# First-layer shift columns on TensorE, fewer GpSimd splits, and four memory units at each change of stage

## The chip, the cores and the metric

One core of one Trainium2 chip runs the whole program as one launch. The metric is the device time in microseconds of that core. Engines go by their names: TensorE (PE, with its weight loads as PEld), VectorE (DVE), ScalarE (ACT), GpSimd (POOL) and SyncE (SP).

## What is computed

Two chained blocks over x of 256 tokens by 1024 channels. The first block has two layers (retention with a PEER feed-forward, then a spatial gating unit with another); each norm is modulated by columns that come from the vector c. The second block adds a hybrid of attention and convolution, cross-attention to a memory, and an MLP. What the change touches is this part (cut):

```python
def rmsnorm(x, gain):
    x32 = x.astype(jnp.float32)
    y = x32 * lax.rsqrt(jnp.mean(x32 * x32, axis=-1, keepdims=True) + EPS)
    return (y * gain.astype(jnp.float32)).astype(x.dtype)

def modulate(h, shift, scale):
    return h * (1 + scale[:, None, :]) + shift[:, None, :]
```

The columns `shift` and `scale` (and four others for each layer) are silu(c) times a 1024 x 6144 matrix `ada_w` plus a bias. The memory's keys and values are projections of the normed memory (256 x 1024), needed only in the second block.

## The kernel before

All activations are held with channels on partitions, as 8 tiles of 128x256. Every weight matrix comes as units of 512 KB (128x1024 f32). `plan` (L204 on) lays them down as one list, in the order in which they are used. `pump` walks the list: it issues loads on SyncE's queue into four `raw` buffers (and eight `early` buffers for the first modulation units), then turns each unit into two halves: ScalarE copies it to the high half (L285), and VectorE, or GpSimd where the plan's `on_pool` marks the unit, subtracts to give the low half (L287). `get` hands a split unit to TensorE; `f1` and `f2` run three fp32r matmuls for each product (L320 to L322, L353 to L355). Up to three split units are held.

An "ada" unit of the list gives one modulation column of 128 channels: VectorE multiplies the 128x1024 unit by `cact`, which is silu(c) in every partition, and sums along the row (L292). After eight of them a bias is added (L296). So eight units make the shift and eight the scale of a norm.

`run` (L536 on) starts the program: it loads `vecs`, `mem`, `craw` (c in every partition) and `x`; ScalarE and VectorE split the memory into `mh` (tiles `h`); `mem_values` runs the eight units `mem_v` into four accumulators `pmv`, with sixteen modulation units of the first layer placed between them in the list. The steps handed to `pipe` run behind each unit: the squares of x and of the memory (`ms_add`, whose sums GpSimd adds at L407), the rotary tables, the root of x. Sums over channels are matmuls with `ones` into `st`.

`retention` begins with `mod_gain` and `apply`: for each of eight tiles VectorE makes `t` (L464), ScalarE the high half of `h` (L465), VectorE the low half (L467). Then come the units `ret_qk` into `pqk`. The memory's root is finished inside retention (`mem_stats`).

The same norm stands at each later change of stage: at `peer(0)`, `sgu` and `peer(1)`. While VectorE and ScalarE work on it, TensorE runs units of `mem_k` (`mem_keys`, into `pmk`): three, three and two. `ms_finish` takes the sum, root and reciprocal behind the first of them. The query units `pq` follow through `f1_pair`.

The order on each engine is the order in which this code issues instructions; nothing is sorted later. DMA issues stand in the queue of the engine that issues them.

Of the kernel before, what the change touches and what calls it, by code (L numbers as in the profile page):

```python
# [10 lines left out]
F32 = mybir.dt.float32  # L11
# [5 lines left out]
AF = mybir.ActivationFunctionType  # L17
# [5 lines left out]
P = 128  # L23
T = 256
D = 1024
# [67 lines left out]
def _layout(x):  # L93
# [10 lines left out]
                                   "g_mlp_2", "g_final_2", "conv_w_2")]  # L104
    o["vecs"] = np.concatenate(vecs, axis=1)
    o["ada"] = x["ada_w"].transpose(0, 2, 1).reshape(2, 48, P, D)
# [39 lines left out]
for _n, _w in (("norm_mix", 16), ("norm_ffn", 16), ("norm_final", 8), ("ada_b", 96), ("sgu_b", 24),  # L146
               ("ln_g", 24), ("ln_b", 24),
               ("g_mix", 8), ("g_attn", 4), ("g_conv", 4), ("g_xattn", 8), ("g_mem", 8), ("g_mlp", 8),
               ("g_final", 8), ("conv_w", 12)):
    VEC[_n] = (_off, _w)  # L150
    _off += _w


class Net:
# [41 lines left out]
    def plan(self):  # L196
# [29 lines left out]
        mk = ws(a["mem_k"], "mem_k")  # L226
# [31 lines left out]
    def pump(self, ahead, spare=None):  # L258
        nc = self.nc
        while self.w_split < self.w_done + ahead and self.n_split < len(self.units):  # L260
            i = self.n_split
            while self.n_load < len(self.units):
# [3 lines left out]
                early = ada and j < 24  # L266
# [12 lines left out]
            self.flying[unit[0] == "ada" and i < 24] -= 1  # L279
# [63 lines left out]
    def f2(self, pss, hs, tag, after=None):  # L343
        mm = self.nc.tensor.matmul
        for q in range(4):
# [49 lines left out]
    def ms_add(self, src):  # L395
# [131 lines left out]
    def run(self):  # L527
# [25 lines left out]
        mem = ps.tile([P, KC, T], F32, name="mem")  # L553
        nc.scalar.dma_start(self.vecs, a["vecs"])
# [8 lines left out]
        iota = ps.tile([P, P], F32, name="iota_all")  # L563
        self.const(iota, "iota")
        self.cs = pf.tile([P, 2, T], F32, name="cs")
        rope = self.rope(ps, self.cs)
# [7 lines left out]
        self.cact = self.p_n.tile([P, D], F32, tag="cact", name="cact")  # L574
        nc.scalar.activation(self.cact, cr, AF.Silu)
        nc.gpsimd.dma_start(self.d_c, self.cact[0:1, :])
        self.ms_begin(KC)
        nc.vector.tensor_copy(self.iota, iota[:, :TOPK])
        nc.vector.tensor_copy(self.iota_rep, iota[:, :, None].to_broadcast([P, P, 2]))
        def squares(src, n):  # L580
            return lambda: [self.ms_add(src[:, n + k]) for k in range(4)]
        st = {}

        def total():
            st[0] = self.ms_root(self.ms_sum(), KC)
            self.ms_begin(KC)

        def rstd():
# [7 lines left out]
        self.fill_pool, self.fill_h = cm_f, mh  # L596
# [14 lines left out]
    def mem_values(self, mh):  # L611
        nc = self.nc
        pss = [self.acc_tile("pmv") for _ in range(4)]
        for g in range(2):
            self.f2(pss[2 * g:2 * g + 2], mh, "mem_v", self.tick)
        self.drain()

        def store(g):
            for tb in range(2):
                o = self.p_n.tile([P, 512], F32, tag="mo", name="mo", bufs=2)  # L620
                nc.scalar.activation(o, pss[2 * g + tb], AF.Copy)
                nc.gpsimd.dma_start(self.d_mv[:, tb, g * 512:g * 512 + 512], o)
        return store

    def mem_keys(self, mh, count, mid=None):
        nc = self.nc
        for k in range(count):
            h = len(self.mem_pend) % 2
            if h == 0:
                self.mem_ps = self.acc_tile("pmk")  # L630
            pt = self.mem_ps[:, h * T:h * T + T]
            self.f1(pt, self.get("mem_k"), mh, mid=mid if k == 0 else None)
            self.mem_pend.append((pt, self.mem_n))
            self.mem_n += 1

    def mem_stores(self):
        nc = self.nc
        while self.mem_pend:
            pt, n = self.mem_pend.popleft()
            o = self.p_n.tile([P, T], F32, tag="mk", name="mk", bufs=3)  # L640
            nc.scalar.activation(o, pt, AF.Copy)
            nc.gpsimd.dma_start(self.d_mk[:, n], o)
# [60 lines left out]
    def retention(self, rstd):  # L703
        nc = self.nc
        gain = self.mod_gain(0, "norm_mix", 8)
        hs = self.apply(rstd, gain, self.mod[0][:, 0:8], {4: lambda: self.mem_store_v(0)})
        self.later.append(lambda: self.mem_store_v(1))
# [119 lines left out]
    def peer(self, l):  # L827
        nc, a = self.nc, self.a
        gain = self.mod_gain(l, "norm_ffn", 32)
        def more():  # L830
            self.mem_keys(self.fill_h, 1)
        self.mem_keys(self.fill_h, 1, self.ms_finish)
        more()
        hs = self.apply(self.rstd, gain, self.mod[l][:, 24:32], {1: more, 6: lambda: self.pump(SPLIT_BUFS)} if l == 0 else {6: lambda: self.pump(SPLIT_BUFS)})
# [87 lines left out]
        def reopen(cm_g):  # L922
# [13 lines left out]
            if l == 0:  # L936
                self.fill_h = self.mem_reload(pf, nc.sync)
# [285 lines left out]
    def sgu(self):  # L1223
        nc, a = self.nc, self.a
        gain = self.mod_gain(1, "norm_mix", 8)
        def more():
            self.mem_keys(self.fill_h, 1)
        self.mem_keys(self.fill_h, 1, self.ms_finish)
        more()
        hs = self.apply(self.rstd, gain, self.mod[1][:, 0:8], {1: more, 6: lambda: self.pump(SPLIT_BUFS)})  # L1230
# [113 lines left out]
        def swap():  # L1344
# [3 lines left out]
            self.fill_h = self.mem_reload(pf, nc.gpsimd)  # L1348
# [446 lines left out]
```

## Time and profile before

| | us |
|---|---|
| median of 3 runs | 2589.46 |
| lowest, highest | 2589.04, 2594.5 |
| profiled execution | 2594.92 |
| its span, first to last instruction | 2593.1 |
| TensorE busy | 2505.1 (97%) |
| VectorE busy | 1905.0 (73%) |
| ScalarE busy | 1258.9 (49%) |
| GpSimd busy | 303.2 (12%) |

The profile is of one execution; its steps are read as durations and starts within the span. A record of a matmul begins before the one ahead of it has ended, so the cost of one in a row is the distance of the starts, not its own length. An fp32 matmul leaves two records. The granted clock of TensorE is given as a share of full speed.

### The profile page before, as it was taken

The page shows a single profiled execution, that of the slowest core. Times are in us where ns is not written, and L with a number is a line of the kernel's source. Part 1 is how long each engine was busy: PE and PEld are TensorE (multiplying, and loading weights), DVE is VectorE, ACT ScalarE, POOL GpSimd, SP SyncE. Part 2 cuts the span into 40 slices and gives each one's busy share as a digit, 9 for nine tenths or more (in the row PEclk, how much of TensorE's full clock was granted, in tenths as well). Part 3 has the DMA queues.
Part 4 walks back from the last instruction along what each step waited for, and adds up shares of the span by engine and source line. Part 5 has one row for each costly group of instructions (what it writes and reads, how often), then busy time and mean ns, then how long its engine had stood idle before and what let it go on. Part 6 is the DMA issues. An engine that isn't in the chain of part 4 may idle for free.

```text
span 2593.1 us, 49906 instructions
## 1 busy us (share of the span) xinstructions
PE 2505.1 (97%) x20358; PEld 2441.9 (94%) x20358; DVE 1905.0 (73%) x3190; ACT 1258.9 (49%) x1790; POOL 303.2 (12%) x210
## 2 busy tenths in 40 slices
PE   5999999999999999999999999999999999989998
PEld 3989999999999999988999999999999999889998
DVE  8777688888868667775776888888675555785754
ACT  4435444444444444455545444444444444665543
POOL 5000312200001000020133222000100000111001
PEclk8999999999999999999999999999999999999999
DMA  7685555555569788867565555555775655444553
GB/s 290 217 300 166 196 174 184 181 182 189 193 219 308 252 301 274 272 224 247 168 203 174 176 183 184 181 190 195 255 249 181 217 187 181 148 134 158 169 193 115
DMA packets 146407, 532.34 MB, mean 205 GB/s; under 512 B 16081, under 2 KB 18257, under 8 KB 145281
## 3 DMA queue, kind: packets, MB, share of 16 engines
q1 hardware_dynamic: 133104, 481.36, 55.9%
q0 software_dynamic: 11584, 45.56, 4.8%
q8 instruction: 160, 2.62, 0.4%
q10 hardware_dynamic: 1488, 2.23, 0.2%
q14 instruction: 71, 0.57, 0.1%
HBM read 506.93 MB, written 22.16 MB: 204 GB/s over the span
## 4 chain that ended last, share of the span: by engine, by line
PE 81%; DVE 9%; DMA 4%; ACT 4%; issue 2%; POOL 1%; DVEq 0%; ACTq 0%; SPq 0%; POOLq 0%
PE pu L320 11%; PE pu L321 11%; PE pu L322 11%; PE V L321 9%; PE V L322 9%; PE V L320 9%; PE po L321 3%; PE po L322 3%; PE po L320 3%; DVE split L287 3%; PE g L1161 2%; ACT split L285 2%; PE pq L321 1%; PE pq L322 1%; PE pq L320 1%
## 5 line engine op out<-in xcount | busy, mean ns | idle before, releaser
L287 DVE TENSOR_TENSOR split<-raw,split 128x1024 fp32r<-128x1024 f32 x740 | 907.9, 1230 | 558.8 <-ACT split L285 558.1
L285 ACT ACTIVATE split<-raw 128x1024 fp32r<-128x1024 f32 x808 | 850.8, 1057 | 711.1 <-PE V L322 334.8
L320 PE MATMUL pu<-h,split 128*128 128x256 f32 x2496 | 718.4, 288 | 0.1
L321 PE MATMUL pu<-h,split 128*128 128x256 f32 x2496 | 706.5, 283 | 0.5 <-DVE h L380 0.5
L322 PE MATMUL pu<-h,split 128*128 128x256 f32 x2496 | 705.9, 283 | 1.1 <-POOL split L287 0.9
L322 PE MATMUL V<-a_sp,split 128*128 128x256 f32 x2048 | 579.9, 283 | 3.6 <-DVE split L287 3.6
L320 PE MATMUL V<-a_sp,split 128*128 128x256 f32 x2048 | 579.9, 283 | 1.2 <-ACT split L285 1.2
L321 PE MATMUL V<-a_sp,split 128*128 128x256 f32 x2048 | 580.1, 283 | 0.1
L321 PEld LDWEIGHTS pu<-h,split 128*128 128x128 f32 x2496 | 478.5, 192 | 1.3 <-DVE h L380 0.7
L322 PEld LDWEIGHTS pu<-h,split 128*128 128x128 f32 x2496 | 478.0, 192 | 1.7 <-POOL split L287 1.3
L320 PEld LDWEIGHTS pu<-h,split 128*128 128x128 f32 x2496 | 478.1, 192 | 0.6 <-ACT u L1328 0.3
L322 PEld LDWEIGHTS V<-a_sp,split 128*128 128x128 f32 x2048 | 393.0, 192 | 4.2 <-DVE split L287 4.2
L320 PEld LDWEIGHTS V<-a_sp,split 128*128 128x128 f32 x2048 | 393.0, 192 | 1.6 <-ACT split L285 1.6
L321 PEld LDWEIGHTS V<-a_sp,split 128*128 128x128 f32 x2048 | 392.9, 192 | 0.5 <-DVE a_sp L374 0.5
L287 POOL TENSOR_TENSOR split<-raw,split 128x1024 fp32r<-128x1024 f32 x68 | 175.3, 2579 | 553.7 <-ACT split L285 551.5
L878 ACT ACTIVATE S<-pu 128x512 f32<-128x512 f32 x128 | 76.5, 597 | 234.8 <-PE pu L322 234.8
L292 DVE SCALAR_TENSOR_TENSOR raw<-raw,cact 128x1024 f32<-128x1024 f32 x96 | 126.8, 1327 | 3.2 <-DMA raw<-in_ada 1.6
L407 POOL TENSOR_TENSOR ms_acc<-ms_acc,sq 128x256 f32<-128x256 f32 x45 | 51.1, 1135 | 571.5 <-ACT sq L405 568.7
L1153 DVE TENSOR_TENSOR og<-og,g 128x512 f16<-128x512 f16 x256 | 108.8, 425 | 8.8
L1171 ACT ACTIVATE stage<-g 128x256 f32<-128x256 f32 x128 | 48.8, 382 | 109.6 <-DVE S L1167 109.6
L320 PE MATMUL pq<-h,split 128*128 128x256 f32 x320 | 95.9, 300 | 3.5 <-ACT h L465 1.9
L321 PE MATMUL pq<-h,split 128*128 128x256 f32 x320 | 93.6, 292 | 4.7 <-DVE h L467 3.2
(370 smaller groups left out, 4018.2 us busy)
## 6 DMA issues: line engine op xcount, KB each, us to landing
raw<-in_pu SPq DMA_DIRECT2D x256, 512.0 KB, 3.3
raw<-in_pv SPq DMA_DIRECT2D x256, 512.0 KB, 4.2
raw<-in_ada SPq DMA_DIRECT2D x96, 512.0 KB, 4.7
raw<-in_pq SPq DMA_DIRECT2D x32, 512.0 KB, 3.3
d_g<-stage POOLq DMA_DIRECT2D x32, 512.0 KB, 3.8
g<-d_g POOLq DMA_DIRECT2D x16, 1024.0 KB, 9.5
raw<-in_mlp_u SPq DMA_DIRECT2D x32, 512.0 KB, 3.4
raw<-in_mlp_d SPq DMA_DIRECT2D x32, 512.0 KB, 4.0
```

The source lines that it names most:

```text
L285: nc.scalar.activation(s[:, 0], r, AF.Copy)
L287: eng.tensor_sub(s[:, 1], r, s[:, 0].bitcast(F32))
L292: nc.vector.scalar_tensor_tensor(r, r, 1.0, self.cact, op0=ALU.mult, op1=ALU.mult, accum_out=self.mod[l][:, o:o + 1])
L320: mm(ps, w_hi, x_hi, start=start, stop=False, **kw)
L321: mm(ps, w_hi, x_lo, start=False, stop=False, **kw)
L322: mm(ps, w_lo, x_hi, start=False, stop=stop, **kw)
L407: nc.gpsimd.tensor_add(self.ms_parts[0], self.ms_parts[0], sq)
L878: nc.scalar.activation(S[:, i - 1:i + 1], pt, AF.Gelu_apprx_tanh)
L1153: nc.vector.tensor_tensor(og[:, k], og[:, 1], pairs(g3[:, k, tt]), op=ALU.mult)
L1161: nc.tensor.matmul(g[:, t], o1[:, t // 2, :, t % 2], og[:, k, t // 2, :, t % 2], start=k == 0, stop=k == 1)
L1171: nc.scalar.activation(stage[0][:, :, k * GT:k * GT + GT], g[:, 64:], AF.Copy)
```

## The change

The first eight units of `ada` are laid out as blocks of matmul weights. They go through ScalarE's DMA queue into a tile `wc` and are multiplied with silu(c) held as a column (`c_col`) by 64 fp32 matmuls with one moving column, into `pmod`; VectorE adds the bias. The scale's eight units stay as they were. At the start only four of the eight `mem_v` units run; the other four run at `peer(0)`, four `mem_k` at `sgu`, and four at `peer(1)`. A new function `bridge` places them. `on_pool` is dropped for the units beside these norms and for `mem_v` and `ret_qk`, and `ms_add` adds on VectorE. At the start the squares come four times as 128x512 into `sq_all`, each root is eight matmuls, and the memory's root is taken there, so that `mem_stats` keeps a reciprocal. The rotary steps `turns` and `reduce` come first.

```diff
-        mix(on_pool(ws(a["mem_v"], "mem_v"), 2, 4, 6), cols(0, 0, 16), 2)
-        mix(on_pool(ws(a["ret_qk"], "ret_qk"), 0, 1, 3))
+        mix(mv[:4], cols(0, 8, 16), 2)
+        mix(ws(a["ret_qk"], "ret_qk"))
...
-        mix(mk[:3])
+        mix(mv[4:])
         for l in range(2):
             pq = ws(a["pq"][16 * l:16 * l + 16], "pq")
-            mix(on_pool(pq, 0, 1, 2, 4, 7, 10, 13))
+            mix(on_pool(pq, 4, 7, 10, 13))
...
-                mix(on_pool(mk[3:6], 2))
-                mix(on_pool(ws(a["sgu_v"], "sgu_v"), 0, 1, 2) + on_pool(ws(a["sgu_u"], "sgu_u"), *range(0, 24, 4)), cols(1, 37, 48), 1, 6)
+                mix(mk[:4])
+                mix(ws(a["sgu_v"], "sgu_v") + on_pool(ws(a["sgu_u"], "sgu_u"), *range(0, 24, 4)), cols(1, 37, 48), 1, 6)
                 mix(ws(a["sgu_o"], "sgu_o", 4))
-                mix(mk[6:8])
+                mix(mk[4:])
...
-            nc.gpsimd.tensor_add(self.ms_parts[0], self.ms_parts[0], sq)
+            nc.vector.tensor_add(self.ms_parts[0], self.ms_parts[0], sq)
...
         nc.scalar.dma_start(self.vecs, a["vecs"])
+        nc.scalar.dma_start(cr, a["c"].to_broadcast([P, D]))
+        rope = self.rope(ps, self.cs)
         for k in range(2):
             nc.sync.dma_start(mem[:, 4 * k:4 * k + 4], a["memT"][:, 4 * k:4 * k + 4])
-        cr = ps.tile([P, D], F32, name="craw")
-        nc.scalar.dma_start(cr, a["c"].to_broadcast([P, D]))
+        nc.scalar.dma_start(wc[:, 0], a["ada"][0])
         nc.scalar.dma_start(self.x, a["xT"])
+        for k in range(1, KC):
+            nc.scalar.dma_start(wc[:, k], a["ada"][k])
...
+        def columns(*ks):
+            for k in ks:
+                w = wc[:, k].rearrange("p (c m) -> p c m", m=P)
+                for c in range(KC):
+                    nc.tensor.matmul(pmod[:, k:k + 1], w[:, c], c_col[:, c:c + 1], start=c == 0, stop=c == KC - 1,
+                                     skip_group_check=True)
...
+        def root():
+            ps = self.st_tile("st")[:, :T]
+            for n in range(KC):
+                nc.tensor.matmul(ps, self.ones, sq[:, n], start=n == 0, stop=n == KC - 1)
+            st[0] = self.ms_root(ps, KC)
...
+        def first():
+            nc.vector.tensor_copy(self.iota, iota[:, :TOPK])
+            nc.vector.tensor_copy(self.iota_rep, iota[:, :, None].to_broadcast([P, P, 2]))
+            columns(1, 2)
+            squares(self.x)
+            rope[2]()
+
+        def second():
+            root()
             self.rstd = self.ms_recip(st[0], "rstd")
-        self.pipe([squares(self.x, 0), lambda: (rope[0](), squares(self.x, 4)()), rope[1],
-                   lambda: (rope[2](), total(), squares(mem, 0)()), rstd, squares(mem, 4)])
-        self.mem_store_v = self.mem_values(mh)
+            columns(3, 4)
+            squares(mem)
+
+        def third():
+            columns(5, 6)
+            root()
+
+        columns(0)
+        self.pipe([first, second, third, lambda: (columns(7), shift())])
+        self.mem_values(mh, 0, self.tick)
...
     def mem_stats(self):
-        r = self.rsqrt(self.ms_sum(), KC, "mrstd")
+        r = self.ms_recip(self.mem_root, "mrstd")
...
+    def bridge(self, gain, shift):
+
+        fill = self.fill
+        fill.popleft()()
+        self.ms_finish()
+        fill.popleft()()
+        hs = self.apply(self.rstd, gain, shift, {1: fill.popleft(), 3: fill.pop(), 6: lambda: self.pump(SPLIT_BUFS)})
+        fill.clear()
+        return hs
```

ScalarE's queue at the start of the program, with the semaphores each instruction waits for. A name such as `DMAHW1` is one of the eight semaphores that all loads of the SyncE and ScalarE queues use in turn. Before:

```order
L554 DMA vecs<-in_vecs 128x268
L558 DMA craw<-in_c 128x1024
L559 DMA x<-in_xT 128x2048
L378 ACT_TABLE_LOAD [waits DMAHW1_49]
L378 ACTIVATE h<-mem,vecs 128x256 [waits DMAHW0_49]
L378 ACTIVATE h<-mem,vecs 128x256 x3
L378 ACTIVATE h<-mem,vecs 128x256 [waits DMAHW3_49]
```

After:

```order
L560 DMA craw<-in_c 128x1024
L564 DMA wc<-in_ada 128x1024
L565 DMA x<-in_xT 128x2048
L567 DMA wc<-in_ada 128x1024 [waits DMAHW1_49]
L567 DMA wc<-in_ada 128x1024 [waits DMAHW3_49]
L567 DMA wc<-in_ada 128x1024 [waits DMAHW5_49]
L567 DMA wc<-in_ada 128x1024 [waits DMAHW7_49]
...
L575 ACT_TABLE_LOAD
L575 ACTIVATE c_col<-vecs 128x8 [waits DMAHW0_49]
L577 ACTIVATE cact<-craw 128x1024 [waits DMAHW2_49]
L379 ACTIVATE h<-mem,vecs 128x256 x8
L286 ACTIVATE split_194<-raw_170 128x1024
```

Seven loads of `wc` (three of them where the dots stand), each with a wait, now stand ahead of the first activation; `c_col` and `cact` moved ahead of the memory's `h`.

VectorE at the first change of stage, from retention to PEER (`x` is the residual, `split` a low half, `rstd` the reciprocal of the root). Before:

```order
L476 SCALAR_TENSOR_TENSOR gain<-mod_80,vecs 128x8
L287 TENSOR_TENSOR split_2538<-raw_2425,split_2538 128x1024
L441 RECIPROCAL rstd<-rs 128x256
L464 SCALAR_TENSOR_TENSOR t<-x,gain,rstd 128x256 x2
L467 SCALAR_TENSOR_TENSOR h<-t,mod_80,h 128x256
L464 SCALAR_TENSOR_TENSOR t<-x,gain,rstd 128x256
```

After:

```order
L477 SCALAR_TENSOR_TENSOR gain<-mod_80,vecs 128x8
L288 TENSOR_TENSOR split_2492<-raw_2378,split_2492 128x1024
L442 RECIPROCAL rstd<-rs 128x256
L288 TENSOR_TENSOR split_2518<-raw_2411,split_2518 128x1024
L465 SCALAR_TENSOR_TENSOR t<-x,gain,rstd 128x256 x2
L468 SCALAR_TENSOR_TENSOR h<-t,mod_80,h 128x256
L288 TENSOR_TENSOR split_2546<-raw_2444,split_2546 128x1024
L465 SCALAR_TENSOR_TENSOR t<-x,gain,rstd 128x256
L468 SCALAR_TENSOR_TENSOR h<-t,mod_80,h 128x256
L465 SCALAR_TENSOR_TENSOR t<-x,gain,rstd 128x256
L468 SCALAR_TENSOR_TENSOR h<-t,mod_80,h 128x256
L288 TENSOR_TENSOR split_2571<-raw_2490,split_2571 128x1024
```

Between the reciprocal and the last `h` stood no split on this engine; now four stand there (three of them shown).

## Rows read from the trace of the kernel before

**Rows 1.** The page's busy shares and its chain that ended last.
```profile
PE 2505.1 (97%) x20358; PEld 2441.9 (94%) x20358; DVE 1905.0 (73%) x3190; ACT 1258.9 (49%) x1790; POOL 303.2 (12%) x210
...
PE 81%; DVE 9%; DMA 4%; ACT 4%; issue 2%; POOL 1%; DVEq 0%; ACTq 0%; SPq 0%; POOLq 0%
```
**Rows 2.** Waits of TensorE, 0 to 130 us: total, times, longest.
```profile
PE pqk L320 <- ACT h L465: 5.6, 1, 5.6
...
PE pqk L322 <- POOL split L287: 1.3, 1, 1.3
```
**Rows 3.** Chain that ended last, 0 to 80 us: start, length, what.
```profile
10.18 10.89 DMA raw<-in_mem_v
...
59.22 2.19 DVE mod L296
61.44 0.18 DVE gain L476
...
62.16 0.52 ACT h L465
```
**Rows 4.** ScalarE's timeline at the start: start, length, operation.
```profile
5.49 1.28 ACT L378 ACT_TABLE_LOAD   x1 [5.49 <-DMA mem<-in_memT]
6.78 1.70 ACT L378 ACTIVATE h<-mem,vecs 128x256 fp32r<-128x256 f32 x4
...
15.62 1.06 ACT L575 ACTIVATE cact<-craw 128x1024 f32<-128x1024 f32 x1
```
**Rows 5.** Waits of SyncE's queue, 0 to 40 us.
```profile
SPq L273 <- DMA craw<-in_c: 3.4, 1, 3.4
```
**Rows 6.** Windows of the start: length, each engine, PEclk, DMA share, GB/s.
```profile
16.00:24.00 8.00, 7.55 (x24) 5.59 (x23) 7.29 (x10) 3.72 (x6) 2.27 (x2) 1.00 1.03 420
...
40.00:48.00 8.00, 5.21 (x14) 3.35 (x12) 8.00 (x11) 6.68 (x13) 4.26 (x4) 0.75 0.47 171
```
**Rows 7.** VectorE's timeline in the start: two modulation units.
```profile
40.88 1.22 DVE L292 SCALAR_TENSOR_TENSOR raw<-raw,cact 128x1024 f32<-128x1024 f32 x1
...
55.79 3.39 DVE L292 SCALAR_TENSOR_TENSOR raw<-raw,cact 128x1024 f32<-128x1024 f32 x1
```
**Rows 8.** TensorE's timeline: memory units at the start, fp16 matmuls in layer 0.
```profile
22.68 0.40 PE L354 MATMUL pmv<-split,h 128*128 128x512 f32 x1
22.91 0.40 PE L355 MATMUL pmv<-split,h 128*128 128x512 f32 x1
...
532.80 0.51 PE L1161 MATMUL g<-og,o 128*128 128x128 f16 x6
533.11 0.36 PE L320 MATMUL pu<-h,split 128*128 128x256 f32 x1
```
**Rows 9.** Chain that ended last, 270 to 300 us, the first change of stage.
```profile
279.67 0.88 PE st L431 x4
...
281.08 1.76 DVE rstd L441
...
285.85 0.48 DVE t L464
286.34 0.41 DVE h L467
...
294.03 2.31 DVE h L467
...
297.61 0.47 PE psr L1013 x4
```
**Rows 10.** Windows of the three changes of stage, columns as in rows 6.
```profile
268.00:300.00 32.00, 28.83 (x222) 27.92 (x221) 22.12 (x27) 16.09 (x28) 14.49 (x12) 0.95 0.51 172
1126.00:1153.00 27.00, 23.75 (x141) 20.20 (x141) 22.32 (x32) 15.54 (x29) 13.33 (x10) 0.94 0.44 154
1362.00:1386.00 24.00, 20.26 (x148) 19.31 (x147) 15.53 (x22) 13.53 (x23) 10.82 (x9) 0.93 0.42 133
```
**Rows 11.** ScalarE's timeline in the gate projection of retention.
```profile
124.48 1.28 ACT L436 ACT_TABLE_LOAD   x1
```

More of the change, by code (lines that the diff above doesn't have):

```diff
@@ L278, in pump @@
             r = self.raw.pop(i)
-            self.flying[unit[0] == "ada" and i < 24] -= 1
+            self.flying[unit[0] == "ada" and i < 16] -= 1
             if unit[0] == "w":
@@ L341, in f1_pair, with f2 @@
                              c == 0 and not (shared and j), c == KC - 1, skip_group_check=True)
-    def f2(self, pss, hs, tag, after=None):
+    def f2(self, pss, hs, tag, after=None, qs=range(4)):
         mm = self.nc.tensor.matmul
-        for q in range(4):
+        for q in qs:
             s = self.get(tag)
@@ L562, in run @@
         self.const(self.ident, "ident")
-        iota = ps.tile([P, P], F32, name="iota_all")
         self.const(iota, "iota")
-        self.cs = pf.tile([P, 2, T], F32, name="cs")
-        rope = self.rope(ps, self.cs)
+        rope[0]()
+        rope[1]()
+        c_col = ps.tile([P, KC], F32, name="c_col")
+        nc.scalar.activation(c_col, self.vec("c"), AF.Silu)
+        self.cact = self.p_n.tile([P, D], F32, tag="cact", name="cact")
+        nc.scalar.activation(self.cact, cr, AF.Silu)
+        nc.gpsimd.dma_start(self.d_c, self.cact[0:1, :])
         self.mem_n = 0
@@ L573, in run @@
         self.pump(1)
[L574 to L581, printed above, removed]
-        st = {}
@@ new lines, in run, with squares @@
+        sq = ps.tile([P, KC, T], F32, name="sq_all")
+        st = {}
+        def squares(src):
+            for n in range(0, KC, 2):
+                nc.scalar.activation(sq[:, n:n + 2].rearrange("p a t -> p (a t)"),
+                                     src[:, n:n + 2].rearrange("p a t -> p (a t)"), AF.Square)
+        def root():
[3 more added lines that the diff above has]
+            st[0] = self.ms_root(ps, KC)
@@ new lines, in shift @@
+        def shift():
+            v0 = VEC["ada_b"][0]
+            nc.vector.tensor_add(self.mod[0][:, :KC], pmod[:, :KC], self.vecs[:, v0:v0 + KC])
+        def first():
[6 more added lines that the diff above has]
+            root()
+            self.rstd = self.ms_recip(st[0], "rstd")
+            columns(3, 4)
+            squares(mem)
@@ L607, in mem_stats, with mem_store_v @@
     def mem_stats(self):
-        r = self.rsqrt(self.ms_sum(), KC, "mrstd")
+        r = self.ms_recip(self.mem_root, "mrstd")
         self.nc.gpsimd.dma_start(self.d_mr, r)
-    def mem_values(self, mh):
+    def mem_store_v(self, g, pss):
         nc = self.nc
[L613 to L633, printed above, removed]
-            self.mem_n += 1
+        for tb in range(2):
+            o = self.p_n.tile([P, 512], F32, tag="mo", name="mo", bufs=2)
+            nc.scalar.activation(o, pss[tb], AF.Copy)
+            nc.gpsimd.dma_start(self.d_mv[:, tb, g * 512:g * 512 + 512], o)
@@ new lines, in mem_values, with mem_value_steps, one @@
+    def mem_values(self, mh, g, after):
+        pss = [self.acc_tile("pmv") for _ in range(2)]
+        self.f2(pss, mh, "mem_v", after)
+        self.later.append(lambda: self.mem_store_v(g, pss))
+    def mem_value_steps(self, mh, g):
+        A = {}
+        def one(q):
+            if q == 0:
+                A["ps"] = [self.acc_tile("pmv") for _ in range(2)]
+            self.f2(A["ps"], mh, "mem_v", None, [q])
+            if q == 3:
+                self.mem_pend.append(lambda: self.mem_store_v(g, A["ps"]))
+        return deque([lambda q=q: one(q) for q in range(4)])
@@ new lines, in mem_key_steps, with one, mem_store_k @@
+    def mem_key_steps(self, mh):
+        A = {}
+        def one(k):
+            n = self.mem_n
+            self.mem_n += 1
+            if k % 2 == 0:
+                A[k] = self.acc_tile("pmk")
+            pt = A[k - k % 2][:, k % 2 * T:k % 2 * T + T]
+            self.f1(pt, self.get("mem_k"), mh)
+            self.mem_pend.append(lambda: self.mem_store_k(n, pt))
+        return deque([lambda k=k: one(k) for k in range(4)])
+    def mem_store_k(self, n, pt):
+        o = self.p_n.tile([P, T], F32, tag="mk", name="mk", bufs=3)
+        self.nc.scalar.activation(o, pt, AF.Copy)
+        self.nc.gpsimd.dma_start(self.d_mk[:, n], o)
@@ L705, in retention @@
         gain = self.mod_gain(0, "norm_mix", 8)
-        hs = self.apply(rstd, gain, self.mod[0][:, 0:8], {4: lambda: self.mem_store_v(0)})
-        self.later.append(lambda: self.mem_store_v(1))
+        hs = self.apply(rstd, gain, self.mod[0][:, 0:8])
         cm_a, pa = self.pool("ret")
@@ L829, in peer @@
         gain = self.mod_gain(l, "norm_ffn", 32)
[L830 to L834, printed above, removed]
+        hs = self.bridge(gain, self.mod[l][:, 24:32])
         pair = [self.acc_tile("pq") for _ in range(2)]
@@ L1225, in sgu @@
         gain = self.mod_gain(1, "norm_mix", 8)
[L1226 to L1230, printed above, removed]
+        hs = self.bridge(gain, self.mod[1][:, 0:8])
         bv, ws, bs = self.sgu_bv, self.sgu_ws, self.sgu_bs
```

34 lines of the change are left out of this document (17 added, 17 removed).

## The prediction

> **What bounds the kernel now.** The page's busy shares and the chain that ended last come first [rows 1]: TensorE is busy 97% of the span and carries 81% of the chain, so a change can win only where TensorE stands idle or runs at the low clock, and costs what it adds to TensorE. Next the waits of TensorE up to 130 us [rows 2]. The start is the one place where it waits for long: it gets its first projection (`pqk`) only at 62.7 us, after eight memory units, and waits 5.6 us in one piece for it. The chain of the start [rows 3] says why: the first weight lands at 21.07, and from 32 us on it runs through VectorE, whose last modulation column (`mod`) is added at 59.22 to 61.41; then come `gain`, `t`, ScalarE's `h`, and `pqk`. So before the change the start ends with VectorE's sixteen modulation units, stretched by GpSimd: a unit takes 1.22 us alone and 3.39 us beside a GpSimd split [rows 7].
>
> **The start, part one: when ScalarE is free.** Eight units become matmul columns, whose weights (`wc`) are loaded from ScalarE's queue ahead of its first arithmetic. The order lists show that the fifth to eleventh load of that queue each wait on a semaphore that another load also uses, eight places back in the two hardware queues; that this costs time can be read in before, where SyncE waits 3.4 us for ScalarE's `craw` to land [rows 5]. ScalarE's last load, wc7, therefore goes out only when wc3 has landed, and all its activations stand behind it: `c_col`, `cact`, the eight `h` of memory, the splits. Queued behind are VectorE (modulation needs `cact`, the low halves need the splits) and TensorE. When is that? In before, the load on the chain landed at 21.07 us [rows 3]. In pieces of 512 KB it was the twelfth: two of `mem`, one `craw`, two of `x`, seven units. In after, wc3 is the fourteenth: the same five, wc0 to wc3, five units. At 420 GB/s [rows 6] a piece takes 0.524/0.420 = 1.25 us, so wc3 lands at 23.6. Before, ScalarE's first arithmetic began at 6.78 [rows 4]. Then follow, by the rows of before, a table load of 1.28, `c_col` (0.25, an estimate), `cact` 1.06, twice 1.70 for `h`, a split of the same size, 1.06 [rows 4]: 30.7. VectorE's low half of 1.22 (the size of an uncontended pass over such a unit [rows 7]) makes it 31.9, when TensorE can run the first memory unit whole.
>
> **Part two: TensorE from there.** Four memory units of twelve matmuls at 0.23 (starts 22.68 and 22.91) [rows 8] are 11.2 us. Two roots of eight fp32 matmuls each, in two records of 0.22 (0.88 for four [rows 9]), are 7.0. The columns have no row of their own: 64 fp32 matmuls of a 128x128 weight against one column, of which 56 stand behind the first unit's start, in 112 records. The nearest row is the fp32 128x128 matmul `psr`: four records in 0.47, 0.118 each [rows 9]. A one-column matmul moves less but must load the same weight. The fp16 128x128 row gives the other side, six in 0.31 (532.80 to 533.11), 0.052 each [rows 8]. I take 0.118, since the weight is fp32 as in the first row: 112 x 0.118 = 13.2; the ends are 5.8 and, if load and matmul don't overlap, twice 0.118 each, 26.4. Sum: 31.9 + 11.2 + 7.0 + 13.2 = 63.3. Behind it the shift's add, gain and `h` need what [rows 3] show from 61.44 to 62.7, 1.3, and about 0.4 for the add: 65.0.
> The Trainium skill ("TensorE: Matmul & The Clock Gate", section Back-to-back issue gap) puts the floor for a moving operand of 1 to 64 columns at about 25 ns; by that the columns would be an estimated 2.8 us. The section LDWEIGHTS of the same page has a load of 128 weight columns take 107 ns, by which they would be an estimated 12.0. No run here separates the two, since every row has at least 128 moving columns.
>
> **Part three: the clock.** The granted clock in before's start was 0.75 of full between 40 and 48 us [rows 6], after a stretch in which TensorE worked 5 of 8 us. After the change its start is again single bursts: columns, which occupy it little, and units that wait for splits. 0.75 means half of a stretch at the lower of the two levels (1.2 and 2.4 GHz). From 32 us on the bursts last about 36; I take a quarter of that at the lower level instead of half, since fewer gaps are left: 9 us, 4.5 lost. First projection: **69.5 instead of 62.7, +7** (VectorE is then no bound: from `cact` at 26, eight units and six splits at 1.22, a reciprocal of 1.75 and copies and rotary steps of some 4 end near 50.) Ends: +2 without a low clock, +20 with columns at 26.4.
>
> **The bridges.** Four units (11.2 us of TensorE) move to the three changes of stage: one more at the first (retention to PEER), one at the second (to SGU), two at the third. Cover for them are TensorE's waits there. In the three windows it is idle 32 - 28.83, 27 - 23.75 and 24 - 20.26: 10.2 us, and the granted clock of 0.95, 0.94, 0.93 loses a further 1.6 + 1.6 + 1.7 = 4.9 [rows 10]. If all were filled, 11.2 - 15.1 = -3.9. What is late next is VectorE, which now does splits itself between `t` and `h`: from the reciprocal's end at 282.84, eight pairs of 0.48 + 0.41 and four splits of 1.23 end at 294.9, against 296.34 before [rows 9], where GpSimd stretched single steps to 2.3 us. So the first bridge ends 1.4 sooner though it holds a unit more; at the second the square sums go over to VectorE, with less gain, and the third has two new units against 3.7 us idle and 1.7 lost. I take **-2**; ends -3.9, and +4 if half of that lost time stays (11.2 - 7.5).
>
> **Splits beside the norm of retention.** TensorE waited 1.3 us for a GpSimd split after `pqk` began [rows 2]; on VectorE, at 1.22, it goes: **-1.3**, ends -1.3 and 0. **Memory's root** is now taken at the start, so the Sqrt in the middle of the gate's Silu falls away with two table loads of 1.28 [rows 11]; that stage has little idle TensorE: **-1**, ends -3 and 0. **Square sums on VectorE** (the adds leave GpSimd) lie under TensorE's matmuls in the output projections: 0, plus or minus 1.
>
> **Sum:** +7 - 2 - 1.3 - 1 = +2.7. The profiled execution took 2594.9 and the span 2593.1, 5.5 over the median of 2589.46; the steps are differences, so they go onto the median: **2592**.
>
> **The rivals.**
> 1. *Columns not covered (slower).* If load and one-column matmul follow each other, or if the columns bring the low clock with them, they take up to 26.4 instead of 13.2. `pqk` then starts at 77 (half of that) to 83, and the time is 2589.5 + 14..20 - 4.3 = 2599 to 2605. It decides from a first projection later than 72.2, with which the sum passes +5.2. For it: the low clock of before's start; against: the fp32 records of `psr` follow each other at 0.118 with their weights loaded among them [rows 9].
> 2. *Columns nearly free (faster).* At the fp16 row's 0.052, with the clock high because there are few idle gaps left: 65.0 - 7.4 = 57.6, -5, with -4.3 from the rest -9.4: 2580. With the low clock kept it is 62.1 and 2585, still inside the forecast's own range. It decides from a first projection before 61.8. For it: a single column moves almost nothing; against it: the fp32 weight. The Trainium skill's floor of the section named first above would make it 55 and an estimated 2577.
> 3. *The queue does not hold ScalarE.* If wc1 to wc7 find their semaphores long done, ScalarE is free near 6 us, the first unit starts at the time of before, 14.4, and TensorE's sum binds: 14.4 + 11.2 + 7.0 + 13.2 + 1.7 + 4.5 = 52, 2574 to 2579 with the units' loads late. Against it: SyncE's 3.4 us. The Trainium skill ("DMA: Bandwidth & Descriptors", section Issuing engines are not separate DMA queues) says that issuing from several engines saves only the sequencer's initiating time, usually small; the trace agrees that it saves nothing in bandwidth (420 GB/s already), and what it may cost ScalarE the page doesn't price.
> 4. *The bridges don't cover (slower).* VectorE's splits delay `h`, and TensorE waits as before: +4 instead of -2, 2598; the point from which it decides is half of the 15.1 us of lost time left.
>
> **How the numbers follow.** A measurement of this kernel tells about 0.2%, 5.2 us, from no change: 2584.3 to 2594.6. Chances: the forecast, near 2592 (own range 2585 to 2595) 0.41; columns not covered 0.27; bridges not covered 0.07; columns nearly free 0.19; queue doesn't hold 0.06. Faster: 0.19 + 0.06 = 0.25; slower: 0.27 + 0.07 = 0.34; same 0.41. Leaving out a tenth at either end, the range is 2579 to 2606.
>
> **What would show it.** Right: ScalarE's first arithmetic near 24 us, the first memory unit near 31, `pmod` records 0.11 apart, first `pqk` at 65 to 73, bridges with under 5 us idle, no GpSimd split in a wait before 300 us. Wrong: `pqk` before 60 or after 75; TensorE at the low clock through the columns; more idle time at a bridge than before; a new wait on VectorE's adds where the sums were GpSimd's.

## The result and the profile after

The changed kernel is slower: a median of 2616.06 us (four runs, 2610.92 to 2620.93) against 2589.25 for the kernel before, a ratio of 1.0098 with a 95% interval of 1.0073 to 1.0124. Beside the experiments it was timed again: 2614.59 (2612.73 to 2617.84) against 2592.02. The forecast was 2592, with a range up to 2606. It missed by 24 us, on the slow side and outside the range.

The profiled execution took 2613.11 us. That is 18.2 above the profiled one of before, while the medians lie 26.8 apart, because before's profiled execution was itself 5.5 above its median and after's 3 below. The steps below explain the 18 us that two traces show.

The page's busy shares and chain, after; [rows 1] are those of before:

```profile
PE 2524.0 (97%) x20510; PEld 2463.1 (94%) x20510; DVE 1890.5 (72%) x3223; ACT 1253.9 (48%) x1780; POOL 211.6 (8%) x149
...
PE 80%; DVE 7%; DMA 6%; ACT 4%; issue 3%; POOL 0%; DVEq 0%; ACTq 0%; SPq 0%; POOLq 0%
```

GpSimd gave up 92 us and VectorE 14; TensorE is busy 19 us longer, since it does more or does it at a lower clock.

Where the time lies is best seen stage by stage. The table takes the starts of certain matmuls from the traces: the first `pqk`; from the end of the output projection (`po`) to the first key scores (`psr`) for the first and third change of stage; from the last `V` to the first `pws` for the second, which holds some 39 us of matmuls of the gating unit (`pv`) as well. The last stage runs from the first `rT` to the last matmul of a root. All numbers are us.

| kernel | first pqk | 1st change | 2nd change | 3rd change | from rT to the last root | median |
|---|---|---|---|---|---|---|
| before | 62.7 | 20.9 | 48.9 | 18.7 | 349.6 | 2589 to 2592 |
| before, second trace | 62.2 | 20.9 | 49.0 | 18.7 | 348.4 | |
| after | 73.2 | 22.5 | 53.8 | 24.6 | 344.8 | 2616.06 |
| after, second trace | 70.2 | 22.5 | 54.2 | 24.4 | 347.4 | 2614.59 |
| e1_mk4 | 74.4 | 22.5 | 51.6 | 23.1 | 346.1 | 2612.27 |
| e2_gp | 59.7 | 23.1 | 54.7 | 24.7 | 345.7 | 2601.86 |
| e3_dve16 | 45.6 | 22.5 | 54.0 | 24.6 | 345.0 | 2586.88 |
| e4_pool | 73.0 | 22.8 | 57.3 | 29.2 | 348.0 | 2624.29 |
| e6_wide | 66.7 | 22.5 | 54.4 | 24.5 | 345.6 | 2609.63 |
| e8_old | 51.6 | 21.6 | 48.3 | 18.3 | 346.5 | 2577.30 |
| e9_msp | 73.8 | 23.8 | 52.2 | 24.5 | 346.5 | 2616.77 |

So the start lost 10.5 us, and the three changes of stage 1.6, 4.9 and 5.9, together 12.4. The other stages sum to a gain of 5. Between the two second traces the start lost 8.0 and the changes of stage 12.5.

**The start.** ScalarE's timeline (start, length, operation) shows its queue held by the seven loads, as forecast; this answers to [rows 4]:

```profile
5.45 18.85 ACTq L567 DMA_DIRECT2D wc<-in_ada  x7
24.33 1.28 ACT L575 ACT_TABLE_LOAD   x1 [24.33 <-DMA wc<-in_ada]
25.63 0.21 ACT L575 ACTIVATE c_col<-vecs 128x8 f32<-128x8 f32 x1
...
29.88 2.93 ACT L286 ACTIVATE split<-raw 128x1024 fp32r<-128x1024 f32 x3
```

TensorE's timeline behind it, with the column groups (`pmod`), the roots (`st`) and the first `pqk`; the memory units stand in the gaps between these rows:

```profile
25.89 3.57 PE L592 MATMUL pmod<-c_col,wc 128*128 128x1 f32 x16 [25.89 <-ACT c_col L575]
...
35.99 4.92 PE L592 MATMUL pmod<-c_col,wc 128*128 128x1 f32 x32
45.52 3.62 PE L606 MATMUL st<-sq_all,ones 128*128 128x256 f32 x16
48.97 4.31 PE L592 MATMUL pmod<-c_col,wc 128*128 128x1 f32 x32
58.41 3.71 PE L592 MATMUL pmod<-c_col,wc 128*128 128x1 f32 x32
61.98 5.37 PE L606 MATMUL st<-sq_all,ones 128*128 128x256 f32 x16
69.98 1.84 PE L592 MATMUL pmod<-c_col,wc 128*128 128x1 f32 x16
73.21 0.58 PE L321 MATMUL pqk<-h,split 128*128 128x256 f32 x1 [1.39 <-ACT h L466]
```

Equal groups take unequal times: 32 column records 4.92 and 3.71, 16 records of a root 3.62 and 5.37. It is the clock: from 32 to 72 us 0.79 of full speed was granted, so it stood at the lower of its two levels for part of this stretch.

**The third change of stage.** VectorE's timeline before, the reciprocal and the last `h` (here and in the next two fences the brackets give the idle time ahead of an instruction and what ended it):

```profile
1368.98 1.75 DVE L441 RECIPROCAL rstd<-rs 128x256 f32<-128x256 f32 x1 [3.65 <-ACT rs L436]
...
1379.79 2.30 DVE L467 SCALAR_TENSOR_TENSOR h<-t,mod,h 128x256 fp32r<-128x256 f32 x1 [0.61 <-ACT h L465]
```

After, with the splits that now stand between the two:

```profile
1382.11 1.75 DVE L442 RECIPROCAL rstd<-rs 128x256 f32<-128x256 f32 x1 [1.73 <-ACT rs L437]
1383.78 1.16 DVE L288 TENSOR_TENSOR split<-raw,split 128x1024 fp32r<-128x1024 f32 x1
...
1387.26 1.23 DVE L288 TENSOR_TENSOR split<-raw,split 128x1024 fp32r<-128x1024 f32 x1 [0.87 <-ACT split L286]
...
1391.32 1.22 DVE L288 TENSOR_TENSOR split<-raw,split 128x1024 fp32r<-128x1024 f32 x1 [1.13 <-ACT split L286]
...
1396.30 1.22 DVE L288 TENSOR_TENSOR split<-raw,split 128x1024 fp32r<-128x1024 f32 x1 [1.12 <-ACT split L286]
...
1398.49 0.49 DVE L468 SCALAR_TENSOR_TENSOR h<-t,mod,h 128x256 fp32r<-128x256 f32 x1 [0.18 <-ACT h L466]
```

The splits that stand among the `t` and `h` cost this chain not 1.23 each but that and a wait of 0.9 to 1.1 for ScalarE's half. From the reciprocal's end (1383.86) to the last `h` (1398.98) it takes 15.1 us; before, with the splits on GpSimd, it took 11.4 (1370.73 to 1382.09). At the first and the second change it is 15.1 too, against 13.5 and 13.6 before. The reciprocal itself ends 6.2 to 6.3 us behind the last `po` at the first and third change in both kernels, and at the first change `psr` starts 1.1 behind the last `h` in both: there VectorE's chain is the whole loss of 1.6. ScalarE right behind the chain of the third change, and TensorE's waits in this window:

```profile
1398.37 0.91 ACT L691 ACTIVATE mk<-pmk 128x256 f32<-128x256 f32 x3
1401.59 0.38 ACT L691 ACTIVATE mk<-pmk 128x256 f32<-128x256 f32 x1 [2.31 <-DMA d_mk<-mk]
1401.87 0.65 ACT L917 ACTIVATE qT<-pq 128x256 f32<-128x256 f32 x2
```
```profile
PE psr L1072 <- ACT qT L917: 2.0, 1, 2.0
PE pq L322 <- DVE h L468: 0.9, 1, 0.9
PE pq L321 <- ACT split L286: 0.9, 1, 0.9
PE pq L323 <- DVE split L288: 0.8, 1, 0.8
```

The fourth copy of a memory key waits 2.31 us for the store of an earlier one, since the tiles `mk` have three buffers and there are now four keys. `qT` stands behind it on ScalarE, and TensorE waits for `qT`. At the second change the same copy waits 2.40 us. Ahead of `pq` TensorE no longer waits (before, it waited 1.9 us there for the first `h`): the units fill that time. Its waits now lie inside `pq`, for `h` and for splits.

### The profile page after: what moved, and what is told of

The parts are those of the page before. It is cut to its first block, busy times and chain, and to the rows that moved or that the text cites. A ratio compares the mean times of both kernels' runs of the same rounds, so it can differ in the third digit from the quotient of the medians.

```text
span 2611.0 us, 50127 instructions
## 1 busy us (share of the span) xinstructions
PE 2524.0 (97%) x20510; PEld 2463.1 (94%) x20510; DVE 1890.5 (72%) x3223; ACT 1253.9 (48%) x1780; POOL 211.6 (8%) x149
## 4 chain that ended last, share of the span: by engine, by line
PE 80%; DVE 7%; DMA 6%; ACT 4%; issue 3%; POOL 0%; DVEq 0%; ACTq 0%; SPq 0%; POOLq 0%
PE pu L321 11%; PE pu L322 11%; PE pu L323 11%; PE V L323 8%; PE V L322 8%; PE V L321 8%; DVE split L288 3%; PE po L322 3%; PE po L323 3%; PE po L321 3%; ACT split L286 2%; PE g L1220 2%; DMA raw<-in_pv 2%; PE pq L322 1%; PE pq L323 1%
## 5 line engine op out<-in xcount | busy, mean ns | idle before, releaser
L288 DVE TENSOR_TENSOR split<-raw,split 128x1024 fp32r<-128x1024 f32 x756 | 925.1, 1227 | 580.6 <-ACT split L286 579.5
L288 POOL TENSOR_TENSOR split<-raw,split 128x1024 fp32r<-128x1024 f32 x52 | 134.5, 2587 | 528.8 <-ACT split L286 528.8
L293 DVE SCALAR_TENSOR_TENSOR raw<-raw,cact 128x1024 f32<-128x1024 f32 x88 | 106.8, 1217 | 1.9 <-DMA raw<-in_ada 1.3
L1230 ACT ACTIVATE stage<-g 128x256 f32<-128x256 f32 x128 | 48.9, 382 | 109.6 <-DVE S L1226 109.6
L321 PE MATMUL pq<-h,split 128*128 128x256 f32 x320 | 95.3, 298 | 2.9 <-ACT split L286 1.6
L322 PE MATMUL pq<-h,split 128*128 128x256 f32 x320 | 92.5, 289 | 3.3 <-DVE h L468 3.1
L323 PE MATMUL pq<-h,split 128*128 128x256 f32 x320 | 91.9, 287 | 1.5 <-DVE split L288 1.5
```

What stands on the lines that cost most here:

```text
L288: eng.tensor_sub(s[:, 1], r, s[:, 0].bitcast(F32))
L293: nc.vector.scalar_tensor_tensor(r, r, 1.0, self.cact, op0=ALU.mult, op1=ALU.mult, accum_out=self.mod[l][:, o:o + 1])
L321: mm(ps, w_hi, x_hi, start=start, stop=False, **kw)
L322: mm(ps, w_hi, x_lo, start=False, stop=False, **kw)
L323: mm(ps, w_lo, x_hi, start=False, stop=stop, **kw)
L1230: nc.scalar.activation(stage[0][:, :, k * GT:k * GT + GT], g[:, 64:], AF.Copy)
```

## The experiments

**e1_mk4.** Four buffers for the stores.

```diff
-        o = self.p_n.tile([P, T], F32, tag="mk", name="mk", bufs=3)
+        o = self.p_n.tile([P, T], F32, tag="mk", name="mk", bufs=4)
```

> The changed kernel with one edit: the tiles into which ScalarE copies memory keys on their way out have four buffers instead of three. Theory A (the fourth key's copy waits for a store to land, ScalarE stands behind it and so do the splits, 2.40 us at the second change of stage and 2.31 at the third, with a low clock behind the third): both waits go, TensorE's start of pws comes 2 to 3 us earlier against the start of pmk and psr at the third change 2 to 4 earlier, the time falls by 4 to 7 us. Rival (VectorE's chain sets the pace of both changes of stage): under 1.5 us.

Measured: 2612.27 us, 2.3 to 3.8 under the two medians of the changed kernel, whose own runs spread over 10 us; the stages show it more clearly than the time. In ScalarE's timeline the four copies now run in one piece, with the next splits right behind:

```profile
1161.85 1.19 ACT L691 ACTIVATE mk<-pmk 128x256 f32<-128x256 f32 x4
1162.91 2.97 ACT L286 ACTIVATE split<-raw 128x1024 fp32r<-128x1024 f32 x3
```

The second change of stage falls from 53.8 to 51.6, the third from 24.6 to 23.1: 3.7 us in the stages. The wait was real and is gone, a little less than the 4 to 7 foreseen. It leaves 1.6, 2.7 and 4.4 us of loss at the three changes of stage, so it is less than half of theirs.

**e2_gp.** The loads wc1 to wc7 move from ScalarE's queue to GpSimd's, behind the memory's `h`.

```diff
-        for k in range(1, KC):
-            nc.scalar.dma_start(wc[:, k], a["ada"][k])
...
         self.pump(1)
+        for k in range(1, KC):
+            nc.gpsimd.dma_start(wc[:, k], a["ada"][k])
```

> The changed kernel with one edit: the loads wc1 to wc7 are issued by GpSimd, behind the memory's h, instead of by ScalarE ahead of its first arithmetic. Theory B (the loads that hold ScalarE until 24.33 us set the start): ScalarE's first arithmetic begins near 6 us, the first memory unit near 14, and the first pqk at 55 to 64 instead of 73.2: 9 to 18 us less. Rival (TensorE's columns, roots and units at the low clock set it, or the loads then come late): first pqk at 68 or later, under 5 us less.

Measured: 2601.86 us, 13 to 14 less, and the first `pqk` at 59.7 instead of 73.2. ScalarE's first arithmetic:

```profile
5.55 0.21 ACT L573 ACTIVATE c_col<-vecs 128x8 f32<-128x8 f32 x1 [1.23 <-DMA vecs<-in_vecs]
9.23 1.06 ACT L575 ACTIVATE cact<-craw 128x1024 f32<-128x1024 f32 x1 [3.47 <-DMA craw<-in_c]
...
13.38 1.04 ACT L286 ACTIVATE split<-raw 128x1024 fp32r<-128x1024 f32 x1
21.17 1.06 ACT L286 ACTIVATE split<-raw 128x1024 fp32r<-128x1024 f32 x1 [6.75 <-DMA raw<-in_mem_v]
```

Theory B holds. The first unit's split moves from 29.88 to 13.38; the later units then wait for their own loads, so not all of these 16.5 us reach `pqk`. Three us of the old start are gained, against before.

**e6_wide.** Each column matmul moves its column 64 times over.

```diff
-                    nc.tensor.matmul(pmod[:, k:k + 1], w[:, c], c_col[:, c:c + 1], start=c == 0, stop=c == KC - 1,
-                                     skip_group_check=True)
+                    nc.tensor.matmul(pmod[:, 64 * k:64 * k + 64], w[:, c], c_col[:, c:c + 1].to_broadcast([P, 64]),
+                                     start=c == 0, stop=c == KC - 1, skip_group_check=True)
...
-            nc.vector.tensor_add(self.mod[0][:, :KC], pmod[:, :KC], self.vecs[:, v0:v0 + KC])
+            nc.vector.tensor_add(self.mod[0][:, :KC], pmod.rearrange("p (k n) -> p k n", n=64)[:, :, 0], self.vecs[:, v0:v0 + KC])
```

> The changed kernel with one edit: each of the 64 column matmuls moves its column 64 times over (64 moving columns instead of one, the same 128x128 weight), and the first of the 64 results is used. Theory E (the one-column matmuls cost their weight load, 0.11 us a record at the high clock, and because they move nothing TensorE's clock falls among them, which the roots and units pay): the column groups take no longer, the clock from 32 to 72 us rises from 0.69 to 0.73 towards 0.9 or more, the first pqk is at 64 to 68 instead of 73.2. Rival (the clock falls because of the waits ahead, or a column costs what it moves): first pqk at 72 or later.

Measured: 2609.63 us, 5 to 6 less, and the first `pqk` at 66.7. The windows from 32 to 72 us (each engine's busy time, then PEclk, DMA share, GB/s), after and e6_wide:

```profile
32.00:72.00 40.00, 39.60 (x191) 34.79 (x191) 17.41 (x28) 11.27 (x18) 0.00 (x0) 0.79 0.31 114
```
```profile
32.00:72.00 40.00, 38.31 (x217) 34.33 (x218) 23.41 (x42) 14.66 (x25) 0.55 (x1) 0.96 0.39 141
```

And the groups of e6_wide, from TensorE's timeline:

```profile
47.27 3.68 PE L592 MATMUL pmod<-c_col,wc 128*128 128x64 f32 x32
53.63 3.68 PE L592 MATMUL pmod<-c_col,wc 128*128 128x64 f32 x32
57.15 3.67 PE L606 MATMUL st<-sq_all,ones 128*128 128x256 f32 x16
```

Theory E holds. With 64 moving columns the granted clock is 0.96, and 32 records take 3.68, as long as with one moving column at the high level (3.71). With one moving column it is 0.79 over the same 40 us, above the 0.69 to 0.73 that the expectation started from, and 0.84 in the second trace. The clock lost 0.21 x 40 = 8.4 us in the changed kernel and 1.6 here; the difference of 6.8 is about what `pqk` gained (6.5). Against the second trace it is 4.8, and `pqk` gained 3.4.

**e3_dve16.** The columns are undone: the plan has sixteen modulation units for VectorE, four to each memory unit, and `wc`, `c_col`, `columns` and `shift` go.

```diff
-        mix(mv[:4], cols(0, 8, 16), 2)
+        mix(mv[:4], cols(0, 0, 16), 4)
...
-        columns(0)
-        self.pipe([first, second, third, lambda: (columns(7), shift())])
+        self.pipe([first, second, third])
```

> The changed kernel with the columns undone: all sixteen modulation units of the first norm go through VectorE as before, four memory units stay at the start, the four others at the changes of stage. Theory C (the columns cost more than the eight VectorE units that they replace, once GpSimd no longer slows VectorE): VectorE's last modulation unit ends at 46 to 52, the first pqk is at 49 to 55, 18 to 24 us less than the changed kernel and 8 to 13 before the kernel before; the whole time is 10 to 22 less than that of the changed kernel. Rival (the start stays bound by VectorE as before): first pqk at 60 to 66, whole time 7 to 13 less.

Measured: 2586.88 us (eleven runs, 2583.41 to 2592.63), 28 to 29 less than the changed kernel, more than the 10 to 22 foreseen; the first `pqk` at 45.6, earlier than foreseen. It is 0.9988 of before (0.9979 to 0.9997). VectorE alone does the sixteen units, the last by 42.0 us, sooner than TensorE does eight of them as columns behind the held queue. It is not the queue alone: e2_gp frees the queue and keeps the columns, and its first `pqk` comes 14.1 later than here. The changes of stage stay as in the changed kernel.

**e8_old.** e3_dve16, with the memory units where they were before: eight `mem_v` at the start, three, three and two `mem_k` later. The edit is shown against e3_dve16.

```diff
-        mix(mv[:4], cols(0, 0, 16), 4)
+        mix(mv, cols(0, 0, 16), 2)
...
-        mix(mv[4:])
+        mix(mk[:3])
...
-                mix(mk[:4])
+                mix(mk[3:6])
...
-                mix(mk[4:])
+                mix(mk[6:8])
```

> e3_dve16 (all sixteen modulation units on VectorE, no GpSimd splits beside the norms, square sums on VectorE) with the memory units placed as before: all eight mem_v at the start, three, three and two mem_k at the changes of stage. Theory F (the four moved units are not covered at the changes of stage, they are added there at nearly their full length, while at the start they stand in time in which TensorE waits for VectorE): the changes of stage fall back to 20 to 21, 49 to 50 and 18 to 20 us, the first pqk is at 49 to 54, the time is 6 to 12 us under e3_dve16. Rival (the splits on VectorE lengthen the changes of stage, whatever the units): they stay at 22 and above, 52 and above, 22 and above, and the time is that of e3_dve16 or more.

Measured: 2577.30 us (2575.14 to 2578.75), a ratio to before of 0.9942 (0.9928 to 0.9955), 9.6 under e3_dve16. It beats both kernels. The changes of stage are 21.6, 48.3 and 18.3, near those of before (20.9, 48.9 and 18.7), though every split beside them is on VectorE. So the rival falls, and the times are about those of theory F: back at the start the four units cost 5.9 us up to the first `pqk`, at the changes of stage they had cost 13.0. That it is their matmuls which are not covered, as theory F says, this run does not show, since a unit takes its split and its store along. The chain of the third change, from VectorE's timeline:

```profile
1355.56 1.75 DVE L441 RECIPROCAL rstd<-rs 128x256 f32<-128x256 f32 x1 [1.73 <-ACT rs L436]
1357.23 1.16 DVE L287 TENSOR_TENSOR split<-raw,split 128x1024 fp32r<-128x1024 f32 x1
...
1365.55 1.23 DVE L287 TENSOR_TENSOR split<-raw,split 128x1024 fp32r<-128x1024 f32 x1 [1.13 <-ACT split L285]
...
1367.75 0.48 DVE L467 SCALAR_TENSOR_TENSOR h<-t,mod,h 128x256 fp32r<-128x256 f32 x1 [0.18 <-ACT h L465]
```

Two splits instead of four stand in it, and it takes 10.9 us (1357.31 to 1368.23) instead of 15.1: some 2.1 for each, the pass and the wait. At the first and the second change there are three, and the chain takes 12.9 us instead of 15.1. The start gains beside this: without GpSimd's splits and adds beside VectorE the sixteen units take 10.6 us less, and the first `pqk` comes 11.1 earlier than before. The two agree, but the other edits of the start (the squares and roots in one go, the order of the first steps) stay in this kernel, and their share was not taken apart. VectorE's modulation units up to 62 us, before and e8_old (busy, mean ns):

```profile
L292 DVE SCALAR_TENSOR_TENSOR raw<-raw,cact 128x1024 f32<-128x1024 f32 x16 | 29.4, 1879 | 0.9 <-ACT cact L575 0.9
```
```profile
L292 DVE SCALAR_TENSOR_TENSOR raw<-raw,cact 128x1024 f32<-128x1024 f32 x16 | 18.8, 1214 | 0.0
```

**e4_pool.** GpSimd splits put back beside the three later norms.

```diff
-            mix(on_pool(pq, 4, 7, 10, 13))
+            mix(on_pool(pq, 0, 1, 2, 4, 7, 10, 13))
...
-                mix(mk[:4])
-                mix(ws(a["sgu_v"], "sgu_v") + on_pool(ws(a["sgu_u"], "sgu_u"), *range(0, 24, 4)), cols(1, 37, 48), 1, 6)
+                mix(on_pool(mk[:4], 3))
+                mix(on_pool(ws(a["sgu_v"], "sgu_v"), 0, 1, 2) + on_pool(ws(a["sgu_u"], "sgu_u"), *range(0, 24, 4)), cols(1, 37, 48), 1, 6)
```

> The changed kernel with the GpSimd splits put back beside the three later norms: units 0 to 2 of each pq, one mem_k, units 0 to 2 of sgu_v. Theory D (VectorE's chain at the changes of stage waits for ScalarE's split before each of its own, 1.1 us each, so the splits on VectorE lengthen the chain): from the reciprocal's end to the last h 11.5 to 13 us instead of 15.1, the time 2 to 6 us less. Rival (GpSimd stretches VectorE's steps to 2.3 us, so that it is no better): within 2 us, or more.

Measured: 2624.29 us, 8 to 10 more, with the second and third change at 57.3 and 29.2. Theory D fell as far as it promised a gain. The third change, VectorE beside GpSimd, and TensorE's wait:

```profile
1391.33 2.68 DVE L465 SCALAR_TENSOR_TENSOR t<-x,gain,rstd 128x256 f32<-128x256 f32 x1
...
1395.94 2.39 DVE L468 SCALAR_TENSOR_TENSOR h<-t,mod,h 128x256 fp32r<-128x256 f32 x1
...
1400.78 2.31 DVE L468 SCALAR_TENSOR_TENSOR h<-t,mod,h 128x256 fp32r<-128x256 f32 x1 [0.61 <-ACT h L466]
```
```profile
1391.34 2.39 POOL L288 TENSOR_TENSOR split<-raw,split 128x1024 fp32r<-128x1024 f32 x1 [14.23 <-DVE h L468]
...
1402.75 0.58 POOL L896 DMA_DIRECT2D d_x<-x  x1
1403.32 1.61 POOL L692 DMA_DIRECT2D d_mk<-mk  x3
```
```profile
PE psr L1072 <- ACT qT L917: 6.6, 1, 6.6
```

Each GpSimd split stretches a VectorE step beside it from 0.48 to 2.3 to 2.7. From the reciprocal's end to the last `h` it is 15.2 us, no less. Worse, the key stores are issued by GpSimd and stand behind its splits, so the fourth copy waits 8.65 us for a buffer instead of 2.31, and `psr` waits 6.6 us instead of 2.0. The second and third change therefore mix two things, and what GpSimd splits would do there with four buffers was not run. The first change has no key to store, and it takes 22.8 us against 22.5: no gain either.

**e9_msp.** The square sums go back to GpSimd.

```diff
-            nc.vector.tensor_add(self.ms_parts[0], self.ms_parts[0], sq)
+            nc.gpsimd.tensor_add(self.ms_parts[0], self.ms_parts[0], sq)
```

> The changed kernel with one edit undone: the square sums of the norms are added on GpSimd again. Theory G (the adds on VectorE are what shortens the last stage, from rT to the last root, 345 to 347 us in the changed kernel against 348 to 350 before): that stage returns to 348 to 350, the changes of stage lengthen by up to 1 us, the time is 2 to 5 us above the changed kernel's 2612 to 2617. Rival (the stage differs by its low-clock stretches alone, and the adds are hidden on either engine): within 2 us.

Measured: 2616.77 us, 0.7 and 2.2 above the two medians of the changed kernel, and the last stage at 346.5. Theory G fell: the last stage does not return to 348 or more. Why it is 0.4 to 5 us shorter than before in all kernels of this study was not found; its low-clock stretches fall at other places in every trace. At the second change the adds do matter: the reciprocal ends 7.6 us behind the last `V` in the changed kernel and 6.7 here, as in before (6.7), and the change takes 52.2 instead of 53.8. The first takes 23.8 instead of 22.5, with its reciprocal and its chain as in the changed kernel, and the whole time shows neither.

**a2 and b2.** The changed kernel and the kernel before, once more.

> The changed kernel once more, beside the others. It took 2610.9 to 2620.9 before; a median of 2612 to 2618 is expected, and by the theory that TensorE's clock in the start decides, the stretches at the low clock before 80 us lie differently in its profile and the first pqk moves by some microseconds with them.

> The kernel before once more, for a second trace, since its first profiled execution took 5.5 us more than its median. Expected: 2588 to 2592, with the missing microseconds in stretches at the low clock, not in the start, which ends by VectorE: first pqk at 62 to 64.

Measured: 2614.59 us for the changed kernel; its first `pqk` is at 70.2 instead of 73.2, with a granted clock of 0.84 from 32 to 72 us instead of 0.79, and its changes of stage are the same within 0.5. So the start of the changed kernel moves by 3 us from run to run with the clock, and the changes of stage do not. The kernel before took 2594.16 in its single run, over what was expected; its stages agree with the first trace within 2 us, its first `pqk` is at 62.2.

## Why the prediction was wrong

**ScalarE's queue: right.** Free at 24.33 against 23.6 forecast, the first unit of TensorE at 30.97 against 30.7. The count of pieces ahead of wc3 was enough.

**The columns' price: right.** 0.118 a record was taken; one-column records at the high level take 1.84/16 = 0.115 in the last group, and one and 64 moving columns cost the same, so what moves is not what a record costs. The Trainium skill ("TensorE: Matmul & The Clock Gate", section LDWEIGHTS) reckons the time of a weight load by its columns alone, an estimated 107 ns for 128 of them, and the trace agrees with a price of that size. The floor of about 25 ns in the Trainium skill (the same page, section Back-to-back issue gap) was not reached in any group here.

**The clock in the start: the term was mis-sized, and its reason was wrong.** 4.5 us were charged. The window from 32 to 72 us shows 8.4 lost, and the 3.9 between the two are the 3.7 between 69.5 and 73.2. I took a quarter of the stretch at the lower level because fewer gaps were left; TensorE had hardly any (it was busy 39.6 of 40 us), and the clock was low all the same. e6_wide shows what it was: the column matmuls with one moving column each brought the clock down. That is one of the two conditions of the first rival, and the first `pqk` lies past its mark of 72.2 in the one trace (73.2) and not in the other (70.2); the 14 to 20 us that the rival put on it did not come.

**The bridges: wrong, and this is the step that failed.** The forecast was -2, with ends of -3.9 and +4; they cost +12.4. The fault lies in the sum of VectorE's chain, eight pairs and four splits of 1.23, 12.0 us from the reciprocal to the last `h`, by which the first bridge was to end 1.4 sooner. The chain took 15.1 us at each of the three changes, and the first bridge ended 1.6 later. The missing 3.1 are three waits of 0.9, 1.1 and 1.1, each for ScalarE's half of the unit that VectorE is to split next. I had the pass of VectorE and left out the hand-over from ScalarE, which stands behind `h` in its own queue. Three bridges make that 9 us over the sum, and against before the chains alone are 1.6, 1.5 and 3.8 longer, 6.9 of the 12.4. Another 3.7 are the stores: four keys on three buffers, a wait that the diff makes (two or three keys became four) and that was not looked for. A further 0.9 is the later reciprocal at the second change. What remains, about 1 us, was not found.

The prediction's cover, TensorE's 15.1 us of idle time and low clock, was not what decided. The memory units did fill the time ahead of the first `pq`, but the end of a bridge follows the last `h`, and each moved unit brings a split into the chain that makes it: 15.1 us with four splits, and in e8_old 12.9 with three and 10.9 with two. Taking the splits off GpSimd was a gain by itself, as forecast but smaller: the chains of e8_old are 0.4 to 0.7 shorter than those of before, which has the same units at each change. That the matmuls of the moved units cost nothing beside this is read from the waits; no run moved a unit without its split. Of the rivals this is the fourth, "the bridges don't cover", by the mechanism that it names, VectorE's splits delaying `h`, and at three times its price; it had a chance of 0.07.

**Retention: about right.** From the first `pqk` to the first `pg` 50.3 became 48.9, the 1.3 of the GpSimd split. From there to the first `py` 73.4 became 72.1 with the memory's root gone from the stage, but the second trace of before has 72.0, so the forecast's -1 is not shown.

**Square sums on VectorE: inside their bounds.** By e9_msp they cost 0.9 at the second change, where 0 with ends of 1 was forecast, and nothing that the whole time shows.

**The sum.** Start +10.5 instead of +7; bridges +12.4 instead of -2; retention -3.0 instead of -2.3; the rest about -2 where 0 was forecast (the last stage -4.8, the one ahead of it +3.6): 18 us between the two traces, where +2.7 was forecast. The other 9 or so between the medians are not of any stage: they come from before's profiled run being a long one and after's a short one; where the runs without a profile differ can't be seen.

## What to carry to other kernels

Idle time of an engine covers moved work only if the work does not delay what the engine is waiting for; read from the trace what ends the wait, here the last `h`, and count what each moved unit adds to the chain that makes it, waits between engines included. A moved unit brings all of its steps along, its split on two engines and its store, and each has to be followed into the queue and the buffers where it lands: count the buffers of every pool whose use per stage goes up. Loads issued from a compute engine's queue can hold that engine for as long as the loads ahead take to land; here that cost 13.5 us up to the first `pqk` (e2_gp), and the eight units that they were meant to spare VectorE take 9.7 (at 1.21 each).

## What the runs showed of the hardware

With fp32 matmuls of one moving column among memory units and roots TensorE was busy by the profile for 39.6 of 40 us, and yet its granted clock was 0.79 (0.84 in a second trace); with 64 moving columns in each of them it was 0.96, at no cost in time for each record (3.71 and 3.68 for 32). ScalarE's queue stood for 18.85 us at seven loads, which the profile does not count as busy time. And a VectorE step of 0.48 us took 2.3 to 2.7 beside a GpSimd split.
